# The weights' low parts and the summed squares of two attention stretches, from VectorE to GpSimd

## The chip, the core and the metric

One core of a Trainium2 chip runs the program. The metric is the device time of one execution in microseconds. The engines are named as the profile names them: PE is TensorE's matmul part, PEld its weight loads, DVE is VectorE, ACT is ScalarE, POOL is GpSimd and SP issues the DMAs.

## The reference

One sequence of 512 tokens of 1024 features goes through two blocks in float32. The first block norms its input, projects it with `w_in`, runs a sparse attention with three branches (compressed, selected, window) and a retention, gates both and merges them. The second is a feed-forward, a mixer (stick-breaking attention and state space heads), an attention over a memory and another feed-forward.

```python
def stick_breaking_attention(q, k, v):
    ...
        z = jnp.einsum('bhtd,bhsd->bhts', qb, kb) * scale
        ...
        log_1mb = jnp.where(causal, jax.nn.log_sigmoid(-z), 0.0)
        suffix = lax.cumsum(log_1mb, axis=3, reverse=True) - log_1mb
        log_a = jnp.where(causal, jax.nn.log_sigmoid(z) + suffix, -jnp.inf)
        a = jnp.exp(log_a)
        outs.append(jnp.einsum('bhts,bhsd->bhtd', a, vb.astype(jnp.float32)))

def hybrid_mixer(u, w_in, conv_w, conv_b, dt_bias, a_log, d_skip, ...):
    ...
    o_att = stick_breaking_attention(heads(q), heads(k), heads(v))
    o_att = o_att.transpose(0, 2, 1, 3).reshape(b_, s_, ATTN_WIDTH)
    o_att = rmsnorm(o_att, attn_norm_g)
    ...
```

## The kernel before

Products with float32 accuracy are made of three faster ones. Every operand x is split into a high part (the upper bits) and a low part (the rest), and a product is high·high + high·low + low·high. For a weight the split has three steps, in `wload`: a DMA brings 128 x 1024 values into `raw` (one of three buffers), ACT copies them rounded into `whi` (line 82), and DVE subtracts, `wlo = raw - whi` (line 83). `whi` and `wlo` have two buffers each. 138 such pieces run through the kernel; PE uses the two parts in groups `(hi, hi), (hi, lo), (lo, hi)`, so the first `wlo` comes two products behind the first `whi`.

The work is written down in the order of the computation, and a scheduler then sets the order on each engine, so that products of a coming projection (lines 158, 203) stand between the steps of the attention. Each engine runs its list in order.

The **first attention stretch** is the sparse attention of the first block, with its projections: keys and values (`ev_kv`, 4 pieces of 1024), window keys and gates (`ev_kw`, 4 pieces of 560), queries (`ev_q`, 4), then `z` (4) and the retention's queries and keys (8), which fill PE while `attention(qi)` runs. An iteration of `attention` (8 per query tile, 32 in all) takes scores from PE, adds the mask and takes the least (line 533, DVE), exponentiates (ACT), forms a factor `c2` of 128 x 2 (lines 536 to 538, DVE), scales (line 540, DVE), transposes on PE, copies the result to SBUF (lines 550, 552, ACT or DVE), and multiplies with the values (line 555, PE).

The **second stretch** is the stick-breaking attention of the mixer, over eight pairs of heads. For each pair `proj_T` makes 128 columns of queries and 128 of keys (2 pieces of weights), and for three groups of query tiles and two heads: scores on PE (line 987), three ACT passes, `l` on DVE (line 994, one input in PSUM), a scan over the keys (line 999, DVE: both inputs, `keep` and `l`, in SBUF), a difference (line 1000, one input in PSUM), an exponential, transposes (line 1006), a copy and the product with the values (line 1015). Behind each pair the outputs are copied (line 1017), squared on ACT, and from the second pair on added to `sq` (line 1023, DVE). After the last pair `sq` is summed over the features by a product with ones.

GpSimd has little to do: `rpow` (line 76, a power of 128 x 1 values) and four copies of 128 x 128 (line 367).

Of the kernel before, what the change touches and what calls it, by code (L numbers as in the profile page):

```python
# [7 lines left out]
F32 = mybir.dt.float32  # L8
F32R = mybir.dt.float32r
AF = mybir.ActivationFunctionType  # L10
ALU = mybir.AluOpType
# [11 lines left out]
# column offsets in the constant arrays  # L23
# [8 lines left out]
def block_kernel(ctx, tc, A, out, upto=99):  # L32
# [28 lines left out]
    def bcast(src, n, tile_):  # L61
        """A vector of n values on every partition."""
        nc.sync.dma_start(tile_, bass.AP(tensor=src.tensor, offset=src.offset, ap=[[0, 128], [1, n]]))
        return tile_
# [6 lines left out]
    def rpow(v, mul, eps, n=1):  # L71
        """(v * mul + eps) ** -0.5 of a [128, n] tile."""
        a = sm.tile([128, 16], F32, name="rp_a", bufs=4)
        V.tensor_scalar(a[:, :n], v, mul, eps, op0=ALU.mult, op1=ALU.add)  # L74
        r = sm.tile([128, 16], F32, name="rp_r", bufs=4)
        POOL.tensor_tensor(r[:, :n], a[:, :n], half[:, :n], op=ALU.pow)  # L76
        return r[:, :n]

    def split(hi, lo, src, scale=None):
        """hi + lo = src (times scale): the upper bits and the rest."""  # L80
        if scale is None:
            ACT.activation(hi, src, AF.Copy)  # L82
            V.tensor_tensor(lo, src, hi.bitcast(F32), op=ALU.subtract)  # L83
        else:
            ACT.activation(hi, src, AF.Copy, scale=scale)
            V.scalar_tensor_tensor(lo, src, scale, hi.bitcast(F32), op0=ALU.mult, op1=ALU.subtract)

# [8 lines left out]
    def wload(src, k0, nk, c0, w, slot=None):  # L96
        raw, _ = wraw(src, k0, nk, c0, w)
        n = nk * w
        hi, lo = slot() if slot else (wp.tile([128, 1024], F32R, name="whi"), wp.tile([128, 1024], F32R, name="wlo"))
        split(hi[:, :n], lo[:, :n], raw[:, :n])  # L100
        return (hi[:, :n].rearrange("p (k c) -> p k c", k=nk), lo[:, :n].rearrange("p (k c) -> p k c", k=nk))

# [1 line left out]
    clock, pend = [0.0], []  # L104

    def tick(n):
        """Counts a product of n columns, and puts in what is due."""
# [13 lines left out]
    def bank(of=(0, 1, 2, 3)):  # L121
        """The next of some PSUM banks for products."""
# [6 lines left out]
    def act_get(pair, k0=0):  # L129
        """Tokens t0..t1 of feature tile k, of activations kept as [128, token tile, k, 128]."""  # L130
# [6 lines left out]
    def proj_T(src, c0, ncols, get, consume, K=8, nt=NT, splits=None, of=(0, 1, 2, 3)):  # L137
        """Features on partitions: for each 128 columns, consume(tile index, [128, tokens] in PSUM)."""
# [25 lines left out]
    def lead_T(groups, get, slots, splits=((0, 2), (2, 4))):  # L164
        """A phase's first two groups of 256 columns (source, column, consume), over the first tokens before the others."""
# [22 lines left out]
    def proj_X(src, c0, w, get, consume, K=8, nt=NT, tail=1, kp=2, korder=None, between=None, slots=()):  # L188
        """Tokens on partitions: for each token tile, consume(t, [128, w] in PSUM)."""
# [31 lines left out]
    def transpose_split(src, n, dst_pair, t, scale=None, k0=0, of=None):  # L221
        """n 128-column tiles of a token tile [128, ., 512], transposed, to hi and lo at [:, t, k0:k0+n]."""
# [28 lines left out]
    def post_pre(src, K, get, g_post, half_scale, g_pre, fg, last=False, dst=None, korder=None, slots=(), tail=1, delay=DELAY):  # L251
        """x += norm(activations @ src) [* 0.5]; returns the next phase's normalised activations."""
# [39 lines left out]
    # =====================================================================  # L292
    # first block
    # =====================================================================
    def first_block():
# [32 lines left out]
        # --- compressed, selected and window keys, values and gates; queries times -1/8  # L328
# [8 lines left out]
        def rope(xv, nh, t):  # L337
            """xv [128, nh, >=16]: rotates its first 16 columns in place."""
# [8 lines left out]
        def doubled(xv, nh):  # L347
            """Each head's 64 columns twice, transposed: [64 | 64 again, head, token] in PSUM."""
# [46 lines left out]

        proj_X(w_in, 512, 512, get, ev_kv)
# [3 lines left out]
        # gates: 1 / (1 + exp(-x))  # L400
# [6 lines left out]
        # --- compressed blocks: the keys' hidden layer on partitions 0 to 63, the values' on 64 to 127  # L407
# [64 lines left out]
        # --- attention, three branches: scores have the sign turned, so that the least is the greatest; outputs as [2 heads x 64, token]  # L472
# [6 lines left out]
        def attention(qi):  # L479
# [4 lines left out]
            # compressed  # L484
# [27 lines left out]
            # selected, window  # L512
# [49 lines left out]
        def ev_zn(j, bank):  # L562
            """2 silu(z) = (tanh(z / 2) + 1) z"""
# [9 lines left out]
        # --- retention  # L573
# [14 lines left out]
        proj_T(w_in, 2328, 512, get, ev_rot(krT), of=(0, 1))  # L588
        oaP = l1.tile([128, 2, NT, 4, 128], F32R, name="oaP", tag="s2")
# [65 lines left out]
        # --- gates of the two branches, in features layout: 2 sigmoid(m) = tanh(m / 2) + 1  # L655
# [10 lines left out]
        # --- outputs of the branches, merged  # L666
# [30 lines left out]
    # =====================================================================  # L697
    # gated feed-forward
    # =====================================================================
# [38 lines left out]
    # =====================================================================  # L738
    # stick-breaking attention and state space heads
    # =====================================================================  # L740
    def mixer(pair, st):
# [7 lines left out]
        # --- convolution over tokens of xs, B and C  # L749
# [38 lines left out]
        # the weights' high and low parts side by side  # L788
# [16 lines left out]
        # --- time steps: softplus(u) = max(u, 0) + log1p(exp(-|u|)), log1p(e) = 2 atanh(e / (2 + e))  # L805
# [32 lines left out]
        # --- cumulated decays of chunk c and head h as rows: high parts on partition 16 c + h, low parts on 64 + 16 c + h, in columns of h  # L838
# [19 lines left out]
        def per_head(v64, c, g):  # L858
            """[128, 8 heads, 64] view of one value per head of a group"""
# [66 lines left out]
        # --- gate 2 silu(z) = (tanh(z / 2) + 1) z, and the norm of each group  # L926
# [21 lines left out]
        # --- stick-breaking attention  # L948
# [6 lines left out]
        # from the last key on: 1e30 up to the query's own key, a restart at the key before it, then the sum  # L955
# [3 lines left out]
        GROUPS = (((0, 0), (1, 128)), ((2, 0),), ((3, 0),))  # L959
        for p in range(8):  # L960
            # queries as [high; low] of a head on the partitions, keys' high parts and low parts on both halves
# [15 lines left out]
            for segs in GROUPS:  # L977
# [32 lines left out]
                # the two first query tiles meet the first keys at once  # L1010
# [9 lines left out]
            else:  # L1020
                q2 = a1.tile([128, 512], F32, name="q2")
                ACT.activation(q2, ob, AF.Square)
                V.tensor_tensor(sq, sq, q2, op=ALU.add)
# [3 lines left out]
        # sums over the features, on all partitions; rstd by exp(-ln(v) / 2) and a Newton step  # L1027
# [25 lines left out]
        # the state space half of the rows first  # L1053
# [6 lines left out]
    # =====================================================================  # L1060
    # attention over the memory
    # =====================================================================
    def memory(memT, x1):
        """Keys and values of the memory."""
# [104 lines left out]
def _constants():  # L1169
    """Masks, rotation angles and decays: of the shapes alone."""  # L1170
# [54 lines left out]
```

## Time and profile before

| | |
|---|---|
| three runs, us | 1965.07, 1969.86, 1970.98 (median 1969.86) |
| span of the profiled execution, us (its device time is not listed apart) | 1963.4 |
| PE busy, us (share) | 1917.5 (98%) |
| DVE busy | 1027.1 (52%) |
| ACT busy | 773.2 (39%) |
| POOL busy | 39.2 (2%) |
| first stretch | 20 to 255 us |
| second stretch | 1143 to 1318 us |

The span runs from the first instruction to the last; the device time holds a little more around it. The shares are means over stretches of different kinds, so each stretch is read by itself. A busy PE is not a PE at its peak, since a matmul's record runs on while the next waits.

### The profile page before, as it was taken

What the parts mean: (1) busy time and instruction counts of PE and PEld (TensorE: products, weight loads), DVE (VectorE), ACT (ScalarE), POOL (GpSimd) and SP (SyncE); (2) the same over time, 40 slices, a digit from 0 to 9 for tenths busy, and PEclk for the clock granted to TensorE, in tenths of its full rate; (3) what the DMA queues carried; (4) which work ended last, traced back from release to release, by engine and by line L of the source; (5) the groups of instructions that cost most, each with busy time, mean ns of one, the idle gap of its engine ahead of it and who ended that gap; (6) DMA issues with size and microseconds to landing.
All of it is one profiled execution on the core that took longest, in us unless ns stands there. A gap on an engine that the chain in (4) does not pass through costs nothing.

```text
span 1963.4 us, 24345 instructions
## 1 busy us (share of the span) xinstructions
PE 1917.5 (98%) x9676; PEld 1557.6 (79%) x9676; DVE 1027.1 (52%) x1751; ACT 773.2 (39%) x1332; POOL 39.2 (2%) x66
## 2 busy tenths in 40 slices
PE   7999999999999999999999999999999999999998
PEld 6777788788878888888877777667788888888887
DVE  5578743824563333323668658887464553333223
ACT  4345533223343232223545457775353432323221
POOL 0000000100000000000000000000000000000000
PEclk9999999999999999999999999999999999999999
DMA  7411033232332333324231355542262322333322
GB/s 243 129 44 33 23 97 97 83 100 86 97 101 93 97 96 97 97 97 129 83 87 43 86 135 129 129 118 68 84 192 87 97 65 86 97 97 97 97 97 86
DMA packets 153706, 191.38 MB, mean 97 GB/s; under 512 B 9748, under 2 KB 111480, under 8 KB 153464
## 3 DMA queue, kind: packets, MB, share of 16 engines
q1 hardware_dynamic: 153592, 189.82, 32.4%
q8 instruction: 76, 1.25, 0.3%
q14 instruction: 38, 0.31, 0.0%
HBM read 175.11 MB, written 2.10 MB: 90 GB/s over the span
## 4 chain that ended last, share of the span: by engine, by line
PE 84%; DVE 7%; ACT 2%; POOL 1%; issue 1%; DMA 1%; SPq 0%; POOLq 0%; DVEq 0%; ACTq 0%
PE mm L158 41%; PE mm L203 28%; PE mm L181 3%; PE ob L1015 1%; PE ob L555 1%; POOL rp_r L76 1%; DVE x_sb L273 1%; DVE cs L999 1%; PE tp L1006 1%; DVE h L245 1%; PE ob L896 1%; PE s L530 1%; PE s L1100 1%; DVE fg L266 1%; PE mm L547 1%
## 5 line engine op out<-in xcount | busy, mean ns | idle before, releaser
L83 DVE TENSOR_TENSOR wlo<-raw,whi 128x1024 fp32r<-128x1024 f32 (+1 forms) x276 | 335.8, 1217 | 652.4 <-ACT whi L82 647.1
L82 ACT ACTIVATE whi<-raw 128x1024 fp32r<-128x1024 f32 (+1 forms) x276 | 291.0, 1055 | 665.4 <-PE mm L203 282.1
L158 PE MATMUL mm<-a_hi,wlo 128*128 128x512 f32 x1120 | 439.9, 393 | 2.0 <-DVE wlo L83 1.9
L158 PE MATMUL mm<-a_hi,whi 128*128 128x512 f32 x1120 | 440.7, 393 | 0.0
L158 PE MATMUL mm<-a_lo,whi 128*128 128x512 f32 x1120 | 440.3, 393 | 0.0
L158 PEld LDWEIGHTS mm<-a_hi,wlo 128*128 128x128 f32 x1120 | 210.4, 188 | 45.5 <-DVE wlo L83 2.7
L158 PEld LDWEIGHTS mm<-a_hi,whi 128*128 128x128 f32 x1120 | 210.4, 188 | 43.5 <-issue 1.4
L158 PEld LDWEIGHTS mm<-a_lo,whi 128*128 128x128 f32 x1120 | 210.5, 188 | 43.2 <-issue 2.6
L203 PE MATMUL mm<-whi,a_hi 128*128 128x512 f32 (+1 forms) x400 | 157.2, 393 | 0.8 <-ACT whi L82 0.8
L203 PE MATMUL mm<-whi,a_lo 128*128 128x512 f32 (+1 forms) x400 | 157.2, 393 | 0.0
L203 PE MATMUL mm<-wlo,a_hi 128*128 128x512 f32 (+1 forms) x400 | 155.6, 391 | 0.0
L203 PE MATMUL mm<-whi,hid_hi 128*128 128x512 f32 x288 | 112.0, 389 | 0.0
L203 PE MATMUL mm<-whi,hid_lo 128*128 128x512 f32 x288 | 112.0, 389 | 0.0
L203 PE MATMUL mm<-wlo,hid_hi 128*128 128x512 f32 x288 | 112.0, 389 | 0.0
L203 PEld LDWEIGHTS mm<-whi,a_hi 128*128 128x128 f32 x400 | 75.7, 189 | 18.1 <-issue 2.5
L203 PEld LDWEIGHTS mm<-whi,a_lo 128*128 128x128 f32 x400 | 75.8, 189 | 15.9 <-issue 2.5
L203 PEld LDWEIGHTS mm<-wlo,a_hi 128*128 128x128 f32 x400 | 75.1, 188 | 15.0 <-issue 1.9
L76 POOL TENSOR_TENSOR rp_r<-rp_a,half 128x1 f32<-128x1 f32 (+1 forms) x58 | 37.1, 640 | 1894.0 <-DVE rp_a L74 1568.5
L203 PEld LDWEIGHTS mm<-whi,hid_hi 128*128 128x128 f32 x288 | 54.1, 188 | 11.2
L203 PEld LDWEIGHTS mm<-whi,hid_lo 128*128 128x128 f32 x288 | 54.1, 188 | 11.2
L203 PEld LDWEIGHTS mm<-wlo,hid_hi 128*128 128x128 f32 x288 | 54.1, 188 | 11.2
L82 ACT ACTIVATE hid_hi<-sg 128x512 fp32r<-128x512 f32 x44 | 27.4, 623 | 61.9 <-DVE sg L720 61.9
(442 smaller groups left out, 2961.4 us busy)
## 6 DMA issues: line engine op xcount, KB each, us to landing
raw<-in_w_in_dram SPq DMA_DIRECT2D x96, 512.0 KB, 3.7
raw<-in_ffn_w_gu_dram SPq DMA_DIRECT2D x88, 512.0 KB, 3.6
raw<-in_ffn_w_down_dram SPq DMA_DIRECT2D x44, 512.0 KB, 3.7
raw<-in_w_out_dram SPq DMA_DIRECT2D x24, 512.0 KB, 3.7
raw<-in_xa_wkv_dram SPq DMA_DIRECT2D x16, 512.0 KB, 3.7
raw<-in_w_ret_o_dram SPq DMA_DIRECT2D x8, 512.0 KB, 3.4
K<-kh SPq DMA_DIRECT2D x32, 128.0 KB, 2.4
K<-kl SPq DMA_DIRECT2D x32, 128.0 KB, 2.3
```

Of the source, the lines that this page charges most:

```text
L76: POOL.tensor_tensor(r[:, :n], a[:, :n], half[:, :n], op=ALU.pow)
L82: ACT.activation(hi, src, AF.Copy)
L83: V.tensor_tensor(lo, src, hi.bitcast(F32), op=ALU.subtract)
L158: PE.matmul(o, a, b, start=(kc + k == 0 and n == 0 and si == 0), stop=(kc + k == K - 1 and n == 2), skip_group_check=True)
L181: PE.matmul(banks[g][j][:, t0 * 128:t1 * 128], a, b, start=(kc + k + n + si == 0), stop=(kc == 1 and k == 3 and n == 2), skip_group_check= ...
L203: PE.matmul(banks[t][:, :w], a, b, start=(kk == 0 and n == 0), stop=(kk == K - 1 and n == 2))
L245: V.scalar_tensor_tensor(h, src, r, g, op0=ALU.mult, op1=ALU.mult)
L266: V.tensor_tensor(fgt, bank, gpost[:, hf * 512:(hf + 1) * 512], op=ALU.mult)
L273: V.scalar_tensor_tensor(xs, fg[:, t if q == 0 else NT + t % 2], r, xs, op0=ALU.mult, op1=ALU.add)
L530: PE.matmul(sbs[e], qS[:, h, qsl], kk[:, br, g, :W], start=(n == 0 and (e == 0 or nk > 2)), stop=(n == 1), skip_group_check=True)
L547: PE.transpose(tp[:, o + j], p[:, e, j * 128:(j + 1) * 128], ident)
L555: PE.matmul(ob[64 * e:64 * e + 64, a], vv[:, j, br, g * 64:(g + 1) * 64], pT[:, e, j], start=False, stop=(br == 1 and j == nk - 1), skip_g ...
```

## The change

Two things move from VectorE to GpSimd. The subtraction of `wload` goes to the engine that stands in `rest[0]`; that is GpSimd from ahead of the keys' and values' projection until the retention's projections are written down, and again during the eight pairs of the mixer. And the sum of squares is made on GpSimd. That is 24 pieces of weights in the first stretch (20 of 128 x 1024, 4 of 128 x 560), and in the second 16 pieces of 128 x 1024 and 7 additions of 128 x 512. All else in the file that differs is comments, left out here.

```diff
-    def split(hi, lo, src, scale=None):
+    def split(hi, lo, src, scale=None, eng=None):
         if scale is None:
             ACT.activation(hi, src, AF.Copy)
-            V.tensor_tensor(lo, src, hi.bitcast(F32), op=ALU.subtract)
+            (eng or V).tensor_tensor(lo, src, hi.bitcast(F32), op=ALU.subtract)
...
+    rest = [V]
+
     def wraw(src, k0, nk, c0, w, raw=None):
...
-        split(hi[:, :n], lo[:, :n], raw[:, :n])
+        split(hi[:, :n], lo[:, :n], raw[:, :n], eng=rest[0])
...
+        rest[0] = POOL
         proj_X(w_in, 512, 512, get, ev_kv)
...
         proj_T(w_in, 2328, 512, get, ev_rot(krT), of=(0, 1))
+        rest[0] = V
...
+        rest[0] = POOL
         for p in range(8):
...
-                V.tensor_tensor(sq, sq, q2, op=ALU.add)
+                POOL.tensor_tensor(sq, sq, q2, op=ALU.add)
+        rest[0] = V
         osT = new_act()
```

The scheduler makes new lists of both programs. POOL's list of before is this from the first norms to the end (`rp_r` is the power of `rpow`):

```order
L76 TENSOR_TENSOR rp_r<-rp_a,half 128x1 x4
L367 COPY vv<-kvt 128x128 x4
L76 TENSOR_TENSOR rp_r<-rp_a,half 128x2 x8
L76 TENSOR_TENSOR rp_r<-rp_a,half 128x1 x46
```

And this is POOL's list of the change from the retention's norms to the fourth pair of heads; `sq` is the sum of squares, and line 1029 was line 1023:

```order
L83 TENSOR_TENSOR wlo<-raw,whi 128x1024 x16
L76 TENSOR_TENSOR rp_r<-rp_a,half 128x2 x8
L76 TENSOR_TENSOR rp_r<-rp_a,half 128x1 x20
L83 TENSOR_TENSOR wlo<-raw,whi 128x1024
L76 TENSOR_TENSOR rp_r<-rp_a,half 128x1 x2
L83 TENSOR_TENSOR wlo<-raw,whi 128x1024
L76 TENSOR_TENSOR rp_r<-rp_a,half 128x1 x2
L83 TENSOR_TENSOR wlo<-raw,whi 128x1024 x7
L1029 TENSOR_TENSOR sq<-sq,q_9377 128x512
L83 TENSOR_TENSOR wlo<-raw,whi 128x1024 x2
L1029 TENSOR_TENSOR sq<-sq,q_9601 128x512
```

The subtractions now share POOL's list with the powers of the norms, and the first two of the mixer stand between four of them. On DVE, before, the list enters the first pair of heads like this (`ql` and `kl` are the low parts of the queries and keys, `l` and `cs` the steps of the scan):

```order
L939 SCALAR_TENSOR_TENSOR zs<-zs,rp_r,gain 128x512
L83 TENSOR_TENSOR wlo<-raw,whi 128x1024
L86 SCALAR_TENSOR_TENSOR ql<-mm,qh 128x512
L83 TENSOR_TENSOR wlo<-raw,whi 128x1024
L83 TENSOR_TENSOR kl<-mm,kh 128x512
L83 TENSOR_TENSOR wlo<-raw,whi 128x1024
L86 SCALAR_TENSOR_TENSOR ql<-mm,qh 128x512
L994 SCALAR_TENSOR_TENSOR l<-s,l 128x384
L999 SCALAR_TENSOR_TENSOR cs<-keep,l 128x128
```

The change has the same place without the subtractions (its lines 944, 1000 and 1005 are 939, 994 and 999 above):

```order
L944 SCALAR_TENSOR_TENSOR zs<-zs,rp_r,gain 128x512
L86 SCALAR_TENSOR_TENSOR ql<-mm,qh 128x512
L83 TENSOR_TENSOR kl<-mm,kh 128x512
L86 SCALAR_TENSOR_TENSOR ql<-mm,qh 128x512
L1000 SCALAR_TENSOR_TENSOR l<-s,l 128x384
L1005 SCALAR_TENSOR_TENSOR cs<-keep,l 128x128
```

Everything else on DVE stays; on PE, ACT and SP no instruction is added or removed, and some change places.

## Rows read from the trace of the kernel before

**Rows 1.** The page's first line: the span.

```profile
span 1963.4 us, 24345 instructions
```

**Rows 2.** Windows: stretch, busy us (instructions) by engine, granted clock, DMA share, GB/s.

```profile
20.00:95.00 75.00, 73.39 (x405) 57.07 (x403) 41.56 (x123) 25.93 (x54) 1.87 (x4) 1.00 0.51 152
95.00:255.00 160.00, 157.26 (x1066) 120.50 (x1066) 123.98 (x416) 79.00 (x197) 0.00 (x0) 1.00 0.14 39
1143.00:1318.00 175.00, 165.78 (x918) 122.49 (x919) 141.62 (x222) 124.20 (x244) 3.42 (x4) 0.98 0.55 136
1298.00:1313.00 15.00, 10.72 (x56) 7.11 (x54) 14.24 (x23) 11.50 (x24) 0.00 (x0) 0.82 0.58 166
```

**Rows 3.** Chain that ended last, shares by line, 95 to 255 us.

```profile
by line: PE mm L158 41.0%; PE ob L555 16.8%; PE s L530 8.5%; PE mm L547 6.7%; PE mm L530 4.1%; PE tp L547 4.0%; PE s L489 3.3%; ACT pT L550 2.7%; PE ob L510 2.6%; PE tp L355 2.0%; PE mm L489 1.1%; issue 1.0%; PE tp L504 0.6%; ACT p L535 0.6
```

**Rows 4.** The same chain, 1143 to 1318 us.

```profile
by line: PE mm L158 37.3%; PE ob L1015 13.3%; DVE cs L999 9.5%; PE tp L1006 8.0%; DVE l L994 5.3%; PE s L987 3.4%; DVE cs L1000 3.3%; issue 3.3%; PE mm L987 2.7%; ACT l L992 2.2%; ACT l L991 2.0%; PE mm L230 1.8%; DVE wlo L83 1.4%; ACT l L9
```

**Rows 5.** Groups on DVE, 20 to 95 us: xcount, busy us, mean ns, idle before.

```profile
L83 DVE TENSOR_TENSOR wlo<-raw,whi 128x1024 fp32r<-128x1024 f32 x9 | 11.0, 1222 | 14.9 <-ACT whi L82 14.9
L83 DVE TENSOR_TENSOR wlo<-raw,whi 128x560 fp32r<-128x560 f32 x4 | 3.0, 738 | 5.2 <-ACT whi L82 5.2
```

**Rows 6.** Groups on DVE, 95 to 255 us.

```profile
L83 DVE TENSOR_TENSOR wlo<-raw,whi 128x1024 fp32r<-128x1024 f32 x11 | 13.4, 1223 | 7.1 <-ACT whi L82 7.1
L540 DVE TENSOR_SCALAR p<-p,c 128x512 f32<-128x512 f32 x16 | 7.1, 481 | 0.1
```

**Rows 7.** Groups on DVE, 1143 to 1330 us.

```profile
L83 DVE TENSOR_TENSOR wlo<-raw,whi 128x1024 fp32r<-128x1024 f32 x17 | 20.7, 1216 | 11.9 <-ACT whi L82 11.9
L999 DVE TENSOR_TENSOR_SCAN cs<-keep,l 128x512 f32<-128x512 f32 x14 | 16.8, 1209 | 0.0
L999 DVE TENSOR_TENSOR_SCAN cs<-keep,l 128x384 f32<-128x384 f32 x16 | 15.1, 943 | 0.0
L999 DVE TENSOR_TENSOR_SCAN cs<-keep,l 128x256 f32<-128x256 f32 x16 | 10.7, 666 | 0.0
L999 DVE TENSOR_TENSOR_SCAN cs<-keep,l 128x128 f32<-128x128 f32 x16 | 6.7, 417 | 0.2
L1023 DVE TENSOR_TENSOR sq<-sq,q 128x512 f32<-128x512 f32 x6 | 4.1, 682 | 1.6 <-ACT q L1022 1.6
```

**Rows 8.** POOL in order of time: start, us, instruction, idle before.

```profile
38.87 0.32 POOL L367 COPY vv<-kvt 128x128 f32<-128x128 f32 x1 [21.26 <-ACT kvt L364]
40.23 0.67 POOL L367 COPY vv<-kvt 128x128 f32<-128x128 f32 x1 [1.04 <-ACT kvt L364]
1423.53 0.55 POOL L76 TENSOR_TENSOR rp_r<-rp_a,half 128x1 f32<-128x1 f32 x1 [3.33 <-DVE rp_a L74]
1427.05 1.46 POOL L76 TENSOR_TENSOR rp_r<-rp_a,half 128x1 f32<-128x1 f32 x1 [2.97 <-DVE s L269]
```

**Rows 9.** DVE in order of time beside two of those.

```profile
40.18 0.56 DVE L350 COPY dbl<-kvt 128x768 f32<-128x768 f32 x1
40.66 0.28 DVE L342 TENSOR_TENSOR rp<-kvt,cb_t 128x32 f32<-128x32 f32 x1
41.37 0.19 DVE L342 TENSOR_TENSOR rp<-kvt,cb_t 128x32 f32<-128x32 f32 x1
1426.89 1.22 DVE L83 TENSOR_TENSOR wlo<-raw,whi 128x1024 fp32r<-128x1024 f32 x1
```

**Rows 10.** ACT, DVE and PE around the last pair's weights, in order of time.

```profile
1283.47 1.06 ACT L82 ACTIVATE whi<-raw 128x1024 fp32r<-128x1024 f32 x1
1288.51 1.21 DVE L83 TENSOR_TENSOR wlo<-raw,whi 128x1024 fp32r<-128x1024 f32 x1
1289.78 0.49 PE L158 MATMUL mm<-a_hi,wlo 128*128 128x512 f32 x1
```

**Rows 11.** Waits for the moved instructions, 1143 to 1318 us: total, times, longest.

```profile
PEld mm L158 <- DVE wlo L83: 2.7, 2, 2.4
PE mm L158 <- DVE wlo L83: 1.9, 1, 1.9
```

## The prediction

> **What bounds the kernel now.** I read the windows first, then the chain that ended last, then DVE's groups, then the order of time around POOL. Over the span of 1963.4 us [rows 1] PE is nearly always busy, and the two stretches of the change are no exception: 157.3 of 160 us in the first's main part and 165.8 of 175 in the second [rows 2]. DVE, a spare engine elsewhere, has 124.0 of 160 and 141.6 of 175 us of work there, and POOL none and 3.4 [rows 2]. So DVE is relieved where it is fullest, and the question is what of that PE notices. In the first stretch the chain is PE's: of the lines it lists down to 0.6%, two are ACT's and none is DVE's [rows 3]. In the second DVE holds 9.5 + 5.3 + 3.3 + 1.4 = 19.5% of it [rows 4], 34 us of 175. [...]
>
> **What leaves DVE.** From 17 to 95 us 10 pieces of 1024 columns (nine in the row, one starts just ahead of the window) at 1.22 us and 4 of 560 at 0.74 [rows 5]: 15.2 us. From 95 to 255 us 10 pieces (the row has 11, the last belongs to the next projection and stays) at 1.22 [rows 6]: 12.2 us. In the second stretch 16 pieces (the 17th is of `w_out` and stays) at 1.216 and 6 additions at 0.682 [rows 7], 19.5 + 4.1 = 23.6 us; the seventh addition comes behind the window.
>
> **What POOL pays.** The trace has no POOL instruction of this size. From below, a subtraction of 1024 columns costs DVE's 1.22 us; from above, eight times the copy of 128 columns that nothing disturbed, 8 x 0.32 = 2.56 us [rows 8]. I take 2.3 us, near the upper end: the copy's fixed part is counted eight times, but it reads one input and the subtraction two. A piece of 560 is then 1.26 us, an addition of 512 columns 1.15 (0.68 to 1.28). [...] POOL's load is 10 x 2.3 + 4 x 1.26 = 28 us of 78, 23 us of 160 and 16 x 2.3 + 6 x 1.15 = 44 us of 175, so POOL bounds nothing.
>
> **What the two engines cost each other.** This carries the forecast. A lone `rp_r` takes 0.55 us; the one at 1427.05 takes 1.46 [rows 8], because a subtraction runs on DVE from 1426.89 to 1428.11 [rows 9], and it ends 0.40 us behind that. The copy at 40.23 takes 0.67 and not 0.32 [rows 8] beside a DVE copy within SBUF [rows 9]. And DVE is held too: the rotation's product that starts at 40.66, while that POOL copy runs, takes 0.28 us, and the same one 0.7 us later 0.19 [rows 9]. So a POOL instruction and a DVE instruction that reads two SBUF tiles, or copies within SBUF, shut each other out. How long a POOL instruction of 2.3 us would hold DVE the trace can't say: 0.09 us if it is as with the copy, 2.3 if it is for its whole length. [...] I take a hold for the whole length, because POOL's own wait in rows 8 lasted to the end of the DVE instruction.
>
> In the second stretch the scans read two SBUF tiles: 62 of them, 16.8 + 15.1 + 10.7 + 6.7 = 49.3 us of 187 [rows 7]. That is one each 3.0 us, 0.8 us long, with 2.2 us of other work or none between (lines 994, 1000, 1008 and 1017 read PSUM). A POOL instruction that starts at a random point of such a gap holds the next scan for 2.3² / (2 x 2.2) = 1.2 us on the mean, an addition for 1.15² / 4.4 = 0.3. Together 16 x 1.2 + 6 x 0.3 = 21 us. DVE's net there is 23.6 - 21 = **2.6 us saved**; with holds of 0.09 us it is 21.6 saved, with holds as long as POOL works (44 us) 20 lost. From 95 to 255 us line 540 is done at 0.48 us for 512 columns [rows 6], faster than the addition's 0.68 [rows 7], so I count it with the copy as shut out. It comes in 32 pairs, one each 5 us, with some 3.7 us between; that makes 2.3² / 7.4 = 0.7 us per piece, 7 us in all, with 23 as the other end. I take 12, because a subtraction starts when ACT has the high part, often while DVE waits for ACT to form line 536's input: **nothing saved** (11 saved to 11 lost). From 17 to 95 us DVE has 41.6 of 75 us of work [rows 2], so either sign lies in its idle time.
>
> **What PE notices.** DVE's 34 us on the second chain are 24% of its 141.6 us, so 2.6 us saved give 0.6. From 1284 to 1313 us, where DVE sets the pace, two subtractions and one addition go in full, 3.1 us, and 2 x 1.2 + 0.3 = 2.7 come back: 0.4. Waits for low parts: one place in the second stretch cost PE 1.9 us [rows 11]. On POOL a subtraction lasts 1.1 us longer but needn't wait for DVE: the last pair's high part was done at 1284.53, DVE took it up at 1288.51, and PE used it at 1289.78, 0.06 us behind its end [rows 10]. On POOL it ends at about 1286.8. I put 0.6 for both. What else is queued on POOL is `rp_r`: the first two subtractions of the mixer stand between four of them, whose results are needed much later, and those have the earlier inputs. Lengthened subtractions lie behind the lead of two buffers. If that cover were gone, each of 16 would show 1.1 us. The sum: 0.6 + 0.4 + 0.6 = 1.6 us saved. Against the profiled execution that is 1961.8 of 1963.4 us; the median lies 6.5 above that span, so 1969.9 - 1.6 = **1968 us**.
>
> **Rivals.** *The hold is short* (as the 0.09 us): DVE keeps 21.6 us in the second stretch, of which 24% or 5 us are on the chain, all 3.1 at its end, and 1.9 of the waits: 10 saved, **1960 us**; if DVE paced the whole stretch, 21.6, 1948. For it: the only row that shows DVE held. Against it: that copy is too short to hold longer than it did. *The port decides against DVE*: a POOL instruction gets in front of a pair of line 540 or of a scan more often than the gaps say, and PE, whose list is in order, waits for the transposes behind them. With the full hold the first stretch loses 11 us and the second 20; if 24% of the 20 (5 us), half of the 11 and some 3 us at the DVE-paced end arrive, it is 13 more, **1983 us**, all of it 2001. It decides from a mean hold of about 1.6 us per subtraction on, 0.4 above DVE's own cost for it. For it: starts right behind ACT put POOL just ahead of line 536. Against it: the chain of the first stretch has no DVE in its list [rows 3]. [...] *Low parts come late*: PE has two products of some 0.23 us between the first use of a high part and that of its low part. If six of 16 subtractions end 1.1 us too late it is 6 more, **1976 us**. Against it: 1.9 us at one place is all that PE's matmuls waited in before [rows 11].
>
> **Chances.** Cancelled 0.42, with a range of its own of 1962 to 1974; short hold 0.30; against DVE 0.21; late low parts 0.07. A measurement of this kernel can tell 0.3%, 5.9 us, from no change. The first case lies nearly all within it (0.38, and 0.02 on either side), the last at its edge (0.02 within, 0.05 over). So faster 0.32, same 0.40, slower 0.28. A tenth on either side leaves 1950 to 1986.
>
> **What the profile would show.** POOL's group of 36 pieces of 1024 columns near 2.3 us, longer where DVE held it. DVE busy in the second stretch some 3 us less if the hold is whole, some 20 less if it is short: the scans' mean against 0.80 us tells (21 us over 62 scans would make it 1.1), as does line 540's 0.48 in the first stretch. PE's time from 1298 to 1313 and the clock there show whether the end got shorter. The prediction is wrong if the scans keep 0.80 us and the end shrinks, or if lines 540 and 999 grow and waits of PE for DVE's copies grow with them, or if PE's waits for `wlo` exceed the 1.9 us.

## The result and the profile after

The change is slower. Its median is 1992.45 us (1991.89 to 1994.39, four runs) against 1968.96 us of the kernel before (1965.07 to 1970.98), a ratio of 1.0125 with a 95% interval of 1.0112 to 1.0137. By the medians that is 23.5 us, outside the range that was given. The profiled execution took 1992.25 us.

From the page of the change, the span, which answers to [rows 1], and the chain that ended last over the whole program, by engine:

```profile
span 1990.5 us, 24367 instructions
...
PE 74%; DVE 8%; POOL 1%; ACT 1%; issue 1%; DMA 1%; SPq 0%; POOLq 0%; DVEq 0%; ACTq 0%
```

The chain's share of PE was 84% before, that of DVE 7%. The span grew by 27.1 us, 3.6 more than the median. Five places of the program, found in both traces by the start of the same instruction, tell where (us from the span's start):

| place | before | change | behind by |
|---|---|---|---|
| first tanh of `z` (ACT, `zn`) | 107.5 | 116.6 | 9.1 |
| retention's first values (ACT, `vr_hi`) | 317.4 | 335.7 | 18.3 |
| mixer's first gate (ACT, `zs`) | 1111.6 | 1129.6 | 18.0 |
| scaling of the stick-breaking outputs (DVE, `oaF`) | 1350.4 | 1375.2 | 24.8 |
| end of the span | 1963.4 | 1990.5 | 27.1 |

Some 9 us are lost before `z` is projected, 9 while the first attention runs, none in the 794 us from there to the mixer, 7 in the second stretch, and 2 behind it (3.4 us at a granted clock of 0.50 from 1627.9 on). The windows that answer to [rows 2] have their ends moved along (stretch, busy us by engine, granted clock, DMA share, GB/s):

```profile
20.00:103.00 83.00, 75.85 (x400) 59.17 (x400) 37.47 (x112) 25.83 (x54) 28.46 (x17) 0.98 0.45 138
103.00:273.00 170.00, 164.17 (x1069) 124.28 (x1069) 120.93 (x405) 78.74 (x197) 25.55 (x11) 0.97 0.13 35
1161.00:1343.00 182.00, 169.50 (x931) 124.56 (x931) 136.26 (x205) 126.59 (x249) 47.03 (x25) 0.98 0.53 131
64.60:68.00 3.40, 3.40 (x12) 2.92 (x11) 2.46 (x10) 2.05 (x7) 1.16 (x1) 0.50 0.38 136
122.60:132.80 10.20, 8.68 (x42) 7.41 (x43) 8.37 (x35) 3.69 (x15) 2.35 (x1) 0.50 0.19 52
1316.00:1331.00 15.00, 12.08 (x66) 8.50 (x63) 12.64 (x23) 11.14 (x23) 1.29 (x1) 0.88 0.56 158
```

The first number behind the stretch's length is PE. It was idle for 1.6 of 75 us in the lead part and is idle for 7.2 of 83 now; from 2.7 of 160 it went to 5.8 of 170, and from 9.2 of 175 to 12.5 of 182. The clock column tells a second thing: it was 1.00 in both windows of the first stretch. Now 10.2 us from 122.6 on run at 0.50, and another 3.4 us from 64.6 on. There products of 128 x 512 that follow one another start 0.43 us apart (65.65, 66.08, 66.50), and 0.23 at 1.00 (before, 96.70, 96.94, 97.17). If PE sets the pace there, these stretches cost by that at most half their length, 6.8 us, as an estimate. So of the 24.8 us by which the scaling of `oaF` is late, PE's idle time in the three windows makes 12.0 and the clock at most 6.8; the other 6 or more lie in PE's own busy time and were not traced further.

What POOL pays, grouped by shape (count, busy us, mean ns, idle before):

```profile
L83 POOL TENSOR_TENSOR wlo<-raw,whi 128x1024 fp32r<-128x1024 f32 x36 | 89.1, 2480 | 273.2 <-ACT whi L82 255.4 <-PE mm L161 17.8
...
L1029 POOL TENSOR_TENSOR sq<-sq,q 128x512 f32<-128x512 f32 x7 | 9.4, 1347 | 62.8 <-ACT q L1028 59.0 <-DMA K<-kh 3.8
...
L83 POOL TENSOR_TENSOR wlo<-raw,whi 128x560 fp32r<-128x560 f32 x4 | 5.7, 1413 | 10.8 <-ACT whi L82 10.8
```

And what happens beside it on DVE. Two pieces of the change's order of time (start, us, engine, line, operation, tiles), the first in the rotation of the keys, the second in the attention:

```profile
60.64 2.36 POOL L83 TENSOR_TENSOR wlo<-raw,whi 128x1024 fp32r<-128x1024 f32 x1 [3.11 <-ACT whi L82]
...
60.77 2.29 DVE L345 TENSOR_TENSOR rp<-kvt,cb_t 128x32 f32<-128x32 f32 x1 [0.85 <-ACT kvt L382]
...
124.97 2.35 POOL L83 TENSOR_TENSOR wlo<-raw,whi 128x1024 fp32r<-128x1024 f32 x1 [8.73 <-PE mm L161]
125.04 2.31 DVE L540 TENSOR_SCALAR c<-c 128x2 f32<-128x2 f32 x1
```

A product of 128 x 32 values and a `c2` step of 128 x 2 each last until some 0.05 us behind POOL's end. The groups on DVE that stretched most, in the lead part (15 to 103 us) of before and then of the change:

```profile
L342 DVE TENSOR_TENSOR rp<-kvt,cb_t 128x32 f32<-128x32 f32 x12 | 2.4, 202 | 0.9 <-ACT kvt L364 0.8
...
L245 DVE SCALAR_TENSOR_TENSOR hs<-x_in,rp_r,gain 128x1024 f32<-128x1024 f32 x1 | 1.3, 1275 | 0.0
```

```profile
L345 DVE TENSOR_TENSOR rp<-kvt,cb_t 128x32 f32<-128x32 f32 x12 | 6.4, 536 | 14.8 <-ACT kvt L367 13.8 <-ACT kvt L382 0.9
...
L248 DVE SCALAR_TENSOR_TENSOR hs<-x_in,rp_r,gain 128x1024 f32<-128x1024 f32 x1 | 3.4, 3383 | 0.7 <-POOL rp_r L76 0.7
```

And those of the change from 103 to 273 us (before: 164 and 157 ns; 481 in [rows 6]) and in the second stretch (before in [rows 7]):

```profile
L540 DVE TENSOR_SCALAR c<-c 128x2 f32<-128x2 f32 x32 | 8.7, 270 | 4.0 <-ACT p L539 4.0
L542 DVE TENSOR_TENSOR c<-c,gate 128x2 f32<-128x2 f32 x32 | 7.8, 245 | 0.6
...
L544 DVE TENSOR_SCALAR p<-p,c 128x512 f32<-128x512 f32 x16 | 7.1, 483 | 0.2
...
L1005 DVE TENSOR_TENSOR_SCAN cs<-keep,l 128x512 f32<-128x512 f32 x14 | 24.7, 1765 | 0.2
L1005 DVE TENSOR_TENSOR_SCAN cs<-keep,l 128x384 f32<-128x384 f32 x15 | 14.2, 947 | 0.0
L1005 DVE TENSOR_TENSOR_SCAN cs<-keep,l 128x256 f32<-128x256 f32 x16 | 11.8, 736 | 0.0
...
L1005 DVE TENSOR_TENSOR_SCAN cs<-keep,l 128x128 f32<-128x128 f32 x16 | 6.8, 422 | 0.4
```

From here on "held" means this lengthening, summed over DVE's groups that stand in both kernels (mean now less mean before, times the count). It is 17.4 us in the first stretch (8.4 in its lead part, 9.0 from `z` on) and 11.0 in the second, 28.4 in all. So DVE's instructions last 22.6 us less in sum than before, and the program takes 23.5 us more.

PE shows where it meets the holds. Its waits from 20 to 105 us (total, times, longest), before and then the change:

```profile
PE tp L355 <- DVE qS L394: 0.5, 1, 0.5
...
PE ob L440 <- DVE Rk L429: 0.4, 1, 0.4
PE tp L355 <- DVE dbl L350: 0.2, 1, 0.2
```

```profile
PE tp L358 <- DVE dbl L353: 2.5, 2, 2.2
PE tp L358 <- DVE kAB L83: 2.4, 2, 1.7
PE ob L444 <- DVE Rk L433: 1.4, 1, 1.4
```

The duplicated keys `dbl` and the keys' low parts `kAB` aren't lengthened themselves; they stand behind the rotation's held products. Against that, the waits for the moved subtractions in the second stretch are nearly what they were in [rows 11] (PEld's wait and PE's are mostly the same time, seen twice):

```profile
PEld mm L161 <- POOL wlo L83: 3.1, 2, 2.1
...
PE mm L161 <- POOL wlo L83: 2.3, 2, 1.7
```

In the first stretch PE waits once for a moved subtraction, 0.3 us, and behind the last pair once for the sum of squares, 0.6 us. For the high parts of the weights it waits 0.8 us in either kernel.

### The profile page after: what moved, and what is told of

Same layout as the page of the kernel before. It is cut to its first block, busy times and chain, and to the rows that moved or that the text cites. A ratio compares the mean times of both kernels' runs of the same rounds, so it can differ in the third digit from the quotient of the medians.

```text
span 1990.5 us, 24367 instructions
## 1 busy us (share of the span) xinstructions
PE 1929.6 (97%) x9676; PEld 1564.3 (79%) x9676; DVE 1010.6 (51%) x1704; ACT 772.8 (39%) x1332; POOL 142.3 (7%) x113
## 4 chain that ended last, share of the span: by engine, by line
PE 74%; DVE 8%; POOL 1%; ACT 1%; issue 1%; DMA 1%; SPq 0%; POOLq 0%; DVEq 0%; ACTq 0%
PE mm L161 38%; PE mm L206 27%; PE mm L184 3%; PE ob L1021 1%; POOL rp_r L76 1%; DVE x_sb L276 1%; DVE cs L1005 1%; DVE h L248 1%; PE tp L1012 1%; PE ob L901 1%; PE s L1107 1%; DVE fg L269 1%; DVE a_lo L83 1%; PE s L993 0%; DVE l L1000 0%
## 5 line engine op out<-in xcount | busy, mean ns | idle before, releaser
L83 DVE TENSOR_TENSOR wlo<-raw,whi 128x1024 fp32r<-128x1024 f32 x236 | 289.1, 1225 | 614.9 <-ACT whi L82 609.7
L83 POOL TENSOR_TENSOR wlo<-raw,whi 128x1024 fp32r<-128x1024 f32 (+1 forms) x40 | 94.8, 2373 | 284.0 <-ACT whi L82 266.2
```

The source lines that it names most:

```text
L83: (eng or V).tensor_tensor(lo, src, hi.bitcast(F32), op=ALU.subtract)
```

## The experiments

Two theories stood at the start. **The hold** (the port theory of the recorded texts; what the two engines share, no run shows): a POOL instruction stops DVE's two-input and SBUF-to-SBUF instructions for its whole length, and DVE's chain to PE is late by that. **The lateness**: POOL needs 2.5 us for what DVE did in 1.2, and PE waits for low parts. A third question came up under way: what the relief of DVE is worth by itself. Each diff is against the change, unless it says otherwise. Each ratio is to runs of the kernel before on the same chip (medians 1967.31 us for e1, e2, e4 and e5, 1967.55 for e3, e6, e7 and e8, 1966.66 for e9 and 1967.13 for e10 to e12).

### Which part costs what: e1, e2, e3, e8

`e1_first_only` makes the second stretch as before:

```diff
-        rest[0] = POOL
+        rest[0] = V
         for p in range(8):
...
-                POOL.tensor_tensor(sq, sq, q2, op=ALU.add)
+                V.tensor_tensor(sq, sq, q2, op=ALU.add)
```

> The change in the first stretch alone: 24 subtractions on GpSimd, while the mixer keeps its subtractions and sums on VectorE. In the trace of the change the first stretch ends 18.3 us late and the second adds 7. If the two losses are separate, this run is some 18 us (0.9%) slower than before, about 1987. If the loss came from an order of the whole program that only both edits together bring, it is within 5 us of before or over 25 us slower.

Measured: 1984.71 us, ratio 1.0088 (1.0073 to 1.0103), 17.4 us.

`e2_second_only` makes the first stretch as before:

```diff
-        rest[0] = POOL
+        rest[0] = V
         proj_X(w_in, 512, 512, get, ev_kv)
```

> The change in the mixer alone: 16 subtractions and 7 additions on GpSimd. If the losses are separate, some 7 us (0.35%) slower than before, about 1976; with the 1.8 us that the last feed-forward lost to a fall of the granted clock it is 9. If the second stretch by itself gains from the 24 us that leave VectorE, as the forecast's first rival had it, it is 3 to 10 us faster.

Measured: 1974.06 us, ratio 1.0038 (1.0025 to 1.0051), 6.8 us. The two add up to 24.2, the change's 23.5: no dependence of the parts on each other shows.

`e3_sums_only` has the first stretch of e2 and the mixer's weights on DVE, so that only the seven additions are POOL's:

```diff
-        rest[0] = POOL
+        rest[0] = V
         proj_X(w_in, 512, 512, get, ev_kv)
...
-        rest[0] = POOL
+        rest[0] = V
         for p in range(8):
```

> Only the 7 additions of the mixer on GpSimd, 1.35 us each instead of 0.68. VectorE loses 4.8 us of work, and is held by at most 7 reads of 1.35 us. Both theories: within 4 us of before.

Measured: 1968.81 us, ratio 1.0008 (0.9996 to 1.002): no difference that can be told. So the second stretch's loss is that of its 16 subtractions, or nearly all of it.

`e8_lead_only` has the second stretch of e1 and gives the first one back to DVE from the attention on, so that POOL makes the 12 pieces of the keys, values, window keys and queries alone:

```diff
+        rest[0] = V
         ob = attention(0)
```

> The change for the 12 pieces ahead of the attention alone (keys, values, window keys, gates, queries); the 12 beside it and the mixer stay on VectorE. In the trace of the change 8.4 of the first stretch's 18.3 us are lost there. The port theory: 8 us slower than before, 1975, since VectorE's rotation and first norm are held there, where VectorE has idle time but PE waits for each of these steps. The forecast, which gave this part no price: within 3 us of before.

Measured: 1976.6 us, ratio 1.0042 (1.0027 to 1.0057), 9.0 us, and the same lengthening as the change's lead part, some 8.4 us held:

```profile
L345 DVE TENSOR_TENSOR rp<-kvt,cb_t 128x32 f32<-128x32 f32 x12 | 6.4, 537 | 14.8 <-ACT kvt L367 13.9 <-ACT kvt L382 0.8
...
L248 DVE SCALAR_TENSOR_TENSOR hs<-x_in,rp_r,gain 128x1024 f32<-128x1024 f32 x1 | 3.4, 3384 | 0.7 <-POOL rp_r L76 0.7
```

In its profile the first tanh of `z` is 8.3 us late. PE's idle time up to there grew from 2.1 to 7.2 us, and 3.4 us from 65.8 on ran at a clock of 0.51, which by the same estimate makes at most 1.7 more. So the 23.5 us split into 9.0 for the lead part, 17.4 - 9.0 = 8.4 for the first attention, and 6.8 for the mixer, each within some 3 us by the intervals.

### The hold without lateness or relief: e4 and e5

In `e4_twin` DVE does all that it did before; POOL makes each of the 40 subtractions once more, into a tile that nobody reads:

```diff
-        split(hi[:, :n], lo[:, :n], raw[:, :n], eng=rest[0])
+        split(hi[:, :n], lo[:, :n], raw[:, :n])
+        if rest[0] is POOL:
+            twin = wp.tile([128, 1024], mybir.dt.bfloat16, name="twin", bufs=1)
+            POOL.tensor_tensor(twin[:, :n], raw[:, :n], hi[:, :n].bitcast(F32), op=ALU.subtract)
...
-                POOL.tensor_tensor(sq, sq, q2, op=ALU.add)
+                V.tensor_tensor(sq, sq, q2, op=ALU.add)
```

> All work stays on VectorE. Beside each of the 40 subtractions GpSimd makes the same subtraction once more, into a tile that nothing reads (rounded to 16 bits for lack of room). Nothing is relieved, and no product waits for GpSimd. If the port alone makes the loss, this run is slower than its pair with 16 columns by 25 us or more, since VectorE keeps its 47 us of subtractions as well. If lateness of the low parts or the order makes it, the two of the pair are within 5 us.

`e5_twin16` differs from e4 in POOL's columns alone; PE and DVE have the same instructions in the same places:

```diff
-            POOL.tensor_tensor(twin[:, :n], raw[:, :n], hi[:, :n].bitcast(F32), op=ALU.subtract)
+            POOL.tensor_tensor(twin[:, :16], raw[:, :16], hi[:, :16].bitcast(F32), op=ALU.subtract)
```

> As its pair, but GpSimd subtracts only 16 of the columns: the same instructions in the same order on TensorE and VectorE, with a short read on GpSimd. Its distance to before shows what another order and the longer holding of the weights' buffers cost without the port: by the port theory within 5 us of before; by the order theory 10 us or more on either side.

Measured: e4 2005.79 us, ratio 1.02 (1.0174 to 1.0227); e5 1968.03, ratio 1.0005 (0.9996 to 1.0015). POOL's group, the longest scans and the attention's scaling of `p` in e4:

```profile
L106 POOL TENSOR_TENSOR twin<-raw,whi 128x1024 bf16<-128x1024 f32 x36 | 107.2, 2978 | 282.7 <-ACT whi L82 257.0 <-issue 20.6 <-ACT kcA L82 4.2
...
L1008 DVE TENSOR_TENSOR_SCAN cs<-keep,l 128x512 f32<-128x512 f32 x14 | 24.8, 1777 | 0.0
...
L547 DVE TENSOR_SCALAR p<-p,c 128x512 f32<-128x512 f32 x16 | 8.7, 577 | 0.1
```

and in e5:

```profile
L106 POOL TENSOR_TENSOR twin<-raw,whi 128x16 bf16<-128x16 f32 x40 | 30.7, 768 | 333.5 <-ACT whi L82 298.5 <-issue 27.1 <-ACT kcA L82 6.4
...
L1008 DVE TENSOR_TENSOR_SCAN cs<-keep,l 128x512 f32<-128x512 f32 x16 | 19.3, 1213 | 0.1
...
L547 DVE TENSOR_SCALAR p<-p,c 128x512 f32<-128x512 f32 x16 | 7.1, 482 | 0.1
```

With the columns gone the lengthening is gone (42 us held in e4, some 1.5 in e5), and with it 37.8 us. Nothing is relieved and no product waits for POOL's result in either, so the hold alone makes a loss larger than the change's. It is a harder hold than the change's: some 16 of the 42 us fall on DVE's own subtractions and additions, which the change doesn't have there. So DVE's low parts come later too; PE's wait for them grew from 1.9 us in e5 to 3.4 in e4. It isn't proof that the change loses nothing to lateness.

### Shorter holds: e7

In `e7_quarters` POOL subtracts each piece in steps of 256 columns:

```diff
+        if rest[0] is POOL:
+            ACT.activation(hi[:, :n], raw[:, :n], AF.Copy)
+            for s in range(0, n, 256):
+                POOL.tensor_tensor(lo[:, s:min(s + 256, n)], raw[:, s:min(s + 256, n)], hi[:, s:min(s + 256, n)].bitcast(F32), op=ALU.subtract)
...
```

> As the change, with each subtraction cut into four of 256 columns (the narrow pieces into three). One lasts some 0.75 us where the whole lasts 2.37, so a hold of VectorE ends sooner, while a low part is complete later, some 3 us behind its high part. The port theory: each hold is at most a third as long, VectorE slips in between, and the time lies between before and the change, about 1980. The lateness theory: slower than the change, 1995 or more.

Measured: 1985.76 us, ratio 1.0089 (1.0074 to 1.0104), 6.7 us less than the change, with some 17 us held and not 28.4. POOL's group and the longest scans:

```profile
L106 POOL TENSOR_TENSOR wlo<-raw,whi 128x256 fp32r<-128x256 f32 x152 | 117.5, 805 | 265.8 <-ACT whi L104 248.4 <-PE mm L166 9.1 <-ACT pc L504 8.3
...
L1010 DVE TENSOR_TENSOR_SCAN cs<-keep,l 128x512 f32<-128x512 f32 x16 | 20.7, 1300 | 0.2
```

A full piece now takes 4 x 0.805 = 3.2 us on POOL, so the whole low part is complete later than in the change, and yet the time is less. The run doesn't separate the theories as it was meant to, because PE needn't wait for the whole: at the mixer's first piece POOL's quarters run from 1157.33 to 1160.91, and PE's first product with that low part starts at 1158.43.

```profile
1157.33 3.58 POOL L106 TENSOR_TENSOR wlo<-raw,whi 128x256 fp32r<-128x256 f32 x4 [0.34 <-ACT whi L104]
...
1158.43 0.50 PE L166 MATMUL mm<-a_hi,wlo 128*128 128x512 f32 x1 [0.36 <-POOL wlo L106]
```

So PE's waits for low parts fell there as well, from 2.3 to 0.4 us in the second stretch, while in the first they grew from 0.3 to 1.2. In sum that is 1.0 us of the 6.7 gained, so lateness can't be most of the gain. The time stayed above the 1980 that the hold theory named, so not all of the loss follows the held time; the next runs show another part of it.

### Relief without the hold: e6, e9, e10, e11, e12

`e6_zero_low` leaves the low parts of the 40 pieces out; POOL writes zeros in their place, which reads nothing:

```diff
+        if rest[0] is POOL:
+            ACT.activation(hi[:, :n], raw[:, :n], AF.Copy)
+            POOL.memset(lo[:, :n].bitcast(F32), 0.0)
...
```

> As the change, but in the two stretches GpSimd fills the weights' low parts with zeros instead of subtracting (the low parts of 40 pieces are left out of the result; the sums stay on GpSimd). VectorE is relieved of the same 51 us, GpSimd reads nothing for the weights, and no low part is late. It prices the relief alone. If the relief is worth its share on the chain, as the forecast had it, or more, it is 10 us or more faster than before, under 1958; if the subtractions stood in slack of VectorE, within 6 us of before. In either case the port theory has it 20 us or more faster than the change.

Measured: 1970.7 us, ratio 1.0017 (1.0008 to 1.0026): DVE is relieved of 51 us, only some 6 us are held, and the time is 3.2 us more.

`e9_no_low` takes the zeros from one tile that is written at the start, so that no engine does anything for the 40 low parts (the additions are POOL's, as in the change):

```diff
+    zero = constp.tile([128, 512], F32R, name="zero")
+    V.memset(zero.bitcast(F32), 0.0)
...
+        if rest[0] is POOL:
+            ACT.activation(hi[:, :n], raw[:, :n], AF.Copy)
+            return (hi[:, :n].rearrange("p (k c) -> p k c", k=nk), zero[:, None, :w].to_broadcast([128, nk, w]))
...
```

> The 40 subtractions of the two stretches are made by no engine: PE takes a tile of zeros, written once at the start, as the low part of those weights (so those low parts are left out), and the seven additions are GpSimd's. DVE is relieved of the same 51 us as in the change, GpSimd has no 128x1024 work at all, and no low part can be late. If relieving DVE is worth its share of the chain as I had predicted, the time falls by some 5 to 10 us, to 1958 to 1963. If relief is worth nothing because PE sets the pace, the time is that of before, 1965 to 1969, and the 3 us that the run with zeros written by GpSimd cost were the 5.7 us for which its writes held DVE. If that run's 3 us came from the changed order of the instructions, they stay here: 1970 to 1972.

Measured: 1972.05 us, ratio 1.0028 (1.0017 to 1.0038). Even a relief that puts none of the 40 subtractions on another engine made the program 5.4 us slower. Three kernels with the same edit on one part each, the additions on DVE as before, show where. Their diffs are against e9. `e10_no_low_lead` does it for the 12 pieces of the lead part:

```diff
+        rest[0] = V
         ob = attention(0)
...
-        rest[0] = POOL
+        rest[0] = V
         for p in range(8):
```

> Zeros stand for the low parts of the 12 pieces of the keys', values', window keys' and queries' projections alone (their low parts are left out); z's, the retention's and the mixer's subtractions and the sums stay on DVE, and GpSimd gets nothing. In the run that takes all 40 subtractions away the 5 us were lost from 95 to 255 us, with 10 us of granted clock 0.5 there. If the price of relief sits behind the start of the attention, this kernel costs nothing: 1965 to 1969. If a changed order costs a little wherever it is changed, some 1.5 to 2 us are lost here: 1969.

`e11_no_low_att` does it for the 12 pieces of `z` and of the retention's queries and keys:

```diff
-        rest[0] = POOL
+        rest[0] = V
         proj_X(w_in, 512, 512, get, ev_kv)
...
+        rest[0] = POOL
         ob = attention(0)
...
-        rest[0] = POOL
+        rest[0] = V
         for p in range(8):
```

> Zeros stand for the low parts of the 12 pieces of z and of the retention's queries and keys alone, which fill PE while the attention runs; all else stays on DVE. If the price of relief is the half-clock stretch behind the start of the attention, this kernel carries all of it: 1971 to 1973, with 7 to 10 us at granted clock 0.5 between 110 and 200 us. If it is a little everywhere, 1969. If relief in this part is worth something by itself and the loss needs the lead part as well, 1964 to 1967.

`e12_no_low_mix` does it for the mixer's 16:

```diff
-        rest[0] = POOL
+        rest[0] = V
         proj_X(w_in, 512, 512, get, ev_kv)
```

> Zeros stand for the low parts of the mixer's 16 pieces alone; all else, the sums too, stays on DVE. DVE has 19.5 us less in the stretch in which it held a fifth of the chain. If that share told what relief is worth, the time falls by some 5 us, to 1961 to 1963. If the share is the steps of one scan behind the other, which stay, nothing changes: 1965 to 1969.

Measured: e10 1966.33 us, ratio 0.9994 (0.9985 to 1.0002); e11 1972.62, ratio 1.0023 (1.0015 to 1.0032); e12 1966.22, ratio 0.999 (0.9981 to 0.9999). The loss is in e11. Its retention begins 5.4 us late (`vr_hi` at 322.8 and not 317.4), and the windows show what came with it. First before, then e11 (stretch, busy us by engine, granted clock, DMA share, GB/s):

```profile
98.00:113.00 15.00, 15.00 (x86) 11.93 (x84) 9.94 (x17) 6.49 (x11) 0.00 (x0) 1.00 0.13 37
95.00:110.00 15.00, 14.50 (x79) 11.23 (x79) 11.30 (x23) 5.43 (x9) 0.00 (x0) 1.00 0.26 72
110.00:160.00 50.00, 48.25 (x349) 38.38 (x349) 37.79 (x171) 23.87 (x78) 0.00 (x0) 1.00 0.13 36
```

```profile
95.00:110.00 15.00, 15.00 (x82) 11.36 (x81) 9.07 (x19) 5.54 (x9) 0.00 (x0) 1.00 0.21 67
113.60:120.40 6.80, 6.69 (x28) 5.50 (x28) 6.10 (x35) 3.69 (x15) 0.00 (x0) 0.50 0.28 77
195.50:198.90 3.40, 3.40 (x12) 2.57 (x10) 2.00 (x8) 0.80 (x2) 0.00 (x0) 0.50 0.00 0
```

PE ran at 0.50 for 6.8 us from 113.6 on and for 3.4 us from 195.5 on, and it had work nearly all of that time: half of 10.2, by the estimate above, is 5.1 of the 5.4 us in this execution. Over all runs the clock explains less: its mean is 0.9947 in e11's eleven and 0.9962 in the 27 of before, which by the same reckoning makes 3 of the 5.5 us, and the runs of either kernel at 0.996 are still 2.9 us apart (three against ten). PE's busy time ahead of the fall doesn't tell the kernels apart. In e11 PE worked 15.00 of 15 us, but so it did in the kernel before from 98 to 113 us, and the clock stayed at 1.00. The profiles of e6, e7, e1 and the change, which all take these 12 pieces off DVE, have such a stretch between 113 and 134 us, 6.8 to 10.4 us long. In those that leave them on DVE it is 3.4 us (e2, e4, e5) or none (before, e3, e8, e10, e12). What brings the fall stays open, and so does the rest of e11's loss.

Two pairs of runs take the same subtractions off DVE and differ in whether POOL makes them. For the lead part that is 9.0 us slower with POOL's work (e8) and 0.8 faster without it (e10), for the mixer 6.8 slower (e2, whose seven additions cost nothing that can be told by e3) and 0.9 faster (e12). So 9.8 and 7.7 us are the price of POOL's subtractions beside DVE, hold and lateness together.

In the mixer the relief is worth 0.9 us (0.2 to 3.7 by the interval), though DVE's part of the chain shrank. From the mixer's first gate to the scaling of `oaF`, e12 takes 239.1 us and the kernel before 238.8, so the end that was to come at DVE's pace didn't come sooner. The chain of e12 in that stretch, by line (its lines 1005, 1010 and 1011 are 994, 999 and 1000 of before), answers to [rows 4]:

```profile
by line: PE mm L166 42.2%; PE ob L1026 12.1%; PE tp L1017 7.6%; PE s L998 5.6%; DVE cs L1010 4.7%; DMA raw<-in_w_out_dram 3.7%; PE mm L998 3.7%; DVE l L1005 3.5%; issue 3.2%; DVE cs L1011 2.2%; DMA K<-kh 1.8%; ACT l L1002 1.1%; DVE aT L1019
```

The three lines of DVE hold 4.7 + 3.5 + 2.2 = 10.4% and not 9.5 + 5.3 + 3.3 = 18.1%, and PE's projections (42.2% and not 37.3%) and two DMAs (3.7 and 1.8%) have taken their place.

## Why the prediction was wrong

**What POOL pays** was right in size. A subtraction of 1024 columns takes 2.48 us on the mean (2.3 taken, 1.22 to 2.56 as bounds), one of 560 columns 1.41 (1.26), an addition 1.35 (1.15, above its upper end of 1.28). POOL bounds nothing: it works 28.46 of 83, 25.55 of 170 and 47.03 of 182 us.

**The hold for the whole length** was right, against the short hold of 0.09 us, which was the largest rival. The rows at 60.64 and 124.97 us show it, and e4 against e5 shows that it follows POOL's columns. [rows 8] and [rows 9] had it already: the copy on POOL that starts at 40.23 ends at 40.90, and the product that starts at 40.66 ends at 40.94. The 0.09 us were all that was left of that hold, and they gave the short hold no support. In the change it is 2.29 us for a product whose mean before was 0.20.

**The sizes of the holds** were too high, which was an error on the safe side. In the second stretch 21 us were predicted and 11.0 came (the scans' mean went from 0.80 to 0.94 us, not to 1.1); from `z` on 12, and 9.0 came. Line 540's scaling of `p`, which was to carry the latter, kept its 0.48 us, by luck of the places: in e4 it has 0.58. The small steps at lines 536 and 538 were held in its stead. For the lead part no hold was worked out at all, and 8.4 us came.

**The step that failed is the conversion to time**, "What PE notices". It set the time that DVE saves against the time that DVE is held, and turned the net into us of the program by one share: "DVE's 34 us on the second chain are 24% of its 141.6 us, so 2.6 us saved give 0.6". By that rule the measured net of 23.6 - 11.0 = 12.6 us in the mixer would have saved 3 us. It lost 6.8. The two are not the same money:

- *Relief is worth next to nothing here.* e12 takes 19.5 us off DVE in the mixer and gains 0.9; e10 takes 12 pieces off in the lead part and gains nothing that can be told; e11 takes 12 pieces off in the attention and loses 5.5. In the mixer the subtractions had stood where nobody waited for DVE ([rows 4] give them 1.4% of the chain), and the steps that PE does wait for, one scan behind the other, keep their length. The 24% was a share of those steps and was applied to work that isn't among them.
- *A hold strikes just those steps.* The scan, the rotation, the factor `c2` have PE's transposes behind them. e8 held some 8.4 us in the lead part and lost 9.0; e4 held some 40 us more than e5 and lost 37.8. That held and lost time come so near to each other is partly chance: in both cases a part of the loss is the clock's (1.7 us in e8's lead part; in the profile of e4 27.2 us at 0.50, in that of e5 13.6), and some 16 of e4's us are holds of DVE's subtractions and additions. A fixed price of a held microsecond isn't shown.

**The lead part had no price.** "From 17 to 95 us DVE has 41.6 of 75 us of work, so either sign lies in its idle time" is the second failed sentence, and it is the dearest: 9.0 us. DVE's idle time there lay between the steps of a chain that goes from PE to ACT to DVE and back to PE (the waits for `dbl`, `kAB` and `Rk` shown above). Here such idle time hid nothing of the 8.4 us.

**The clock** was looked at in one place alone, the end of the mixer. There nothing became shorter: DVE works 12.64 of 15 us, PE 12.08, at 0.88 ([rows 2]: 14.24, 10.72, 0.82). That DVE sets the pace of this end, from which the sum has its 0.4 us, no run shows: e12, without the 16 subtractions, reaches `oaF` 239.1 us behind the gate, and the kernel before 238.8. Where the clock cost time was in the first stretch, 10.2 us at 0.50 in the attention and 3.4 in the lead part, and that wasn't foreseen.

**The rivals.** *The port decides against DVE* was the right one, with 0.21 and 1983 us. Its condition was wrong: it was to need a mean hold of 1.6 us per subtraction, 0.4 above DVE's own 1.22, and the mean was 28.4 / 40 = 0.7. A condition that sets holds against relief makes the same mistake as the sum. *Low parts come late* has at most a small part: PE's waits for them went from 1.9 to 2.3 us in the mixer, with 0.3 in the first stretch, and for the sum 0.6, so 1.3 us in all. On the chain of the second stretch the subtractions went from 1.4% of 175 us to 2.6% of 182, which is 2.3 us more. That lateness without any hold costs nothing was not tried by itself.

**The signs.** Of the three that the prediction named, the sign of the short hold, scans that keep 0.80 us beside a shorter end, didn't come. The second came in part: line 999 grew and PE's waits for DVE's copies with it (`dbl` from 0.2 to 2.5 us in the lead part, `aT` from 1.7 to 2.8 in the second stretch), but line 540 didn't. The third came barely: PE's waits for `wlo` exceed the 1.9 us by 0.4.

By the runs, the sum is 9.0 (lead part, e8; its relief alone, e10, is worth nothing) + 8.4 (attention; if 5.5 of it are e11's, some 3 are left for the holds, a difference that no run shows alone) + 6.8 (mixer, e2) = 24.2 us, against 23.5 measured. No kernel here is faster than the one before by more than e12's 0.1%, and e12 leaves part of the computation out. So no placing of this move that was tried gains, and for the mixer e12's interval leaves 3.7 us at most.

## What to carry to other kernels

Time that is taken off an engine and time for which it is held are two terms, each with a price of its own: ask which instructions PE waits for, price the relief by whether the removed ones are among them, and the hold by whether it can strike those. A busy share of half an engine, or its share of the chain, prices neither. Before work goes to GpSimd beside a chain of small VectorE steps, put a twin of it there that nobody reads, as in e4, and a short one, as in e5: their distance shows the hold. Here it was an upper end, 37.8 us against the 23.5 of the change, since the work that VectorE kept was held as well.

## What the runs showed of the hardware

- A small instruction was held as well: one of 128 x 2 values, with a mean of 0.16 us before, took 2.31 beside 2.35 us of POOL. In the change neither the reciprocal of the same 128 x 2 values (159 ns before, 161 now) nor the instructions with one input in PSUM (`kAB` at 287 and 286) were lengthened. One reciprocal lies wholly inside a subtraction on POOL, from 216.66 to 216.82 us where POOL works from 216.15 to 218.55, and so does a `kAB` from 66.96 to 67.25 where POOL works from 66.84 to 69.22.
- Zeros written by POOL, which reads nothing for them, left two-input instructions nearly as they were (`rp` 202 ns in both, the longest scans 1217 against 1209) but still lengthened a copy and a scaling within SBUF (`dbl` of 128 x 256 from 292 to 400 ns, `p` of 128 x 128 from 279 to 364). The copy of the keys before, and then in e6 with POOL's group:

```profile
L350 DVE COPY dbl<-kvt 128x256 f32<-128x256 f32 x4 | 1.2, 292 | 0.0
```

```profile
L105 POOL MEMSET wlo<- 128x1024 f32 x36 | 34.5, 962 | 293.0 <-PE mm L165 238.0 <-PE mm L210 54.7 <-POOLq L1224 0.3
...
L357 DVE COPY dbl<-kvt 128x256 f32<-128x256 f32 x4 | 1.6, 400 | 0.2
```

- The granted clock fell to 0.50 for 10.2 us of the first attention in e11, which adds no work to any engine there. It fell behind 15 us in which PE had no gap, and stayed at 1.00 behind 15 such us of the kernel before.
